# Hybrid encoder trunk on one core: four projection tiles instead of three side by side through the rows of x at the front

## The chip, the core and the metric

One Trainium2 chip, one of its cores. The core has TensorE (matmul, in the profile PE, its weight loads PEld), VectorE (DVE), ScalarE (ACT), GpSimd (POOL) and SyncE (SP, here the queue that issues nearly all DMAs), with SBUF and PSUM as its memories. The metric is the device time of one execution in microseconds (us); of a kernel, the median of several runs. One execution is also taken with the hardware profiler, and its span is what the profile divides up.

## The reference

One layer over 528 tokens (16 meta tokens ahead of 512 tokens of x), width 2048. All arithmetic is float32.

```python
h_res = concatenate([meta, x], axis=1)
hn = _rmsnorm(h_res, norm_in_g)
P = hn @ w_in                                   # 2048 x 8320
Pr, Pc = P[..., :RW_COLS], P[..., RW_COLS:]
prev = pad(Pr[:, :-1], one row at the top)
Pr = Pr + (prev - Pr) * mu_shift
r, k, v, g_r, wl, al = parts of Pr              # 4 x 1024, 64, 64
w_raw = -softplus(-(w0 + tanh(wl) @ w_lora_up)) - 0.5
decay = exp(-exp(w_raw)); a = sigmoid(a0 + al @ a_lora_up)
kk = k * k_k, normalised per head; k = k * (1 + (a - 1) * k_a)
y = _rwkv7_recurrence(r, decay, k, v, kk, kk * a)
y_a = (groupnorm(y) * lnx_g + lnx_b + bonus) * silu(g_r)
Bg, Cg, hc, g_c = parts of Pc                   # 4 x 1024
y_b = Bg * _causal_depthwise_conv(Cg * hc, conv_w) * silu(g_c)
h_res = h_res + concatenate([y_a, y_b]) @ w_out
out = _rmsnorm(h_res, norm_f_g)[:, N_META:]
```

The first RMS norm divides each token by a scale that depends on that token alone; the kernel multiplies the projections of the unscaled rows by it afterwards (`rs`).

## The kernel before

**Projections.** `w_in` is cut into 65 column tiles of 128: one of the low-rank inputs ("lora"), eight each of k, r, v, g (the RWKV half) and of B, C, h, gc (the convolution half). `plan` (line 105) is the order in which they are computed; `stream` holds each tile's weights as two halves of 128x1024. x lies transposed as 16 row blocks of 128 (`kt`), with all 528 tokens as columns. A tile is the sum over the 16 blocks, and for each block there are three matmuls: every float32 operand is split into a rounded part and its remainder (xh and xl for x, wh and wl for the weights), and hi x hi, hi x lo and lo x hi are added up in PSUM (`steps`, line 303). A tile's tokens lie in two PSUM banks (`FULL`: 2 x 264 columns, for lora, k, v; `TAIL`: 258 + 256, for r, g, C, h) or, where the meta tokens aren't wanted, in one (`REAL`: 512, for B and gc). So a FULL or TAIL tile takes 96 matmuls, a REAL tile 48 twice as wide.

**Splitting.** For weights ScalarE writes wh and VectorE (for odd quarters later in the stream GpSimd) writes wl = w - wh (`split_w`, lines 121 to 126; a quarter is 128x512 and covers four row blocks). Six buffers each hold wh and wl, three hold raw halves. For x, ScalarE writes xh (with the norm's gain) and VectorE xl (`split_x`, line 191). `square_x` squares a row block on ScalarE and adds it up on VectorE (`accd`, line 203), for the token scale.

**The front.** The first three tiles (lora, k0, r0) go side by side through the row blocks as these arrive: block by block in the first quarter (`quarters` 0, 2, 4, cut into pieces that come with the first blocks of x in one array, `front`), then quarter by quarter. The order of ScalarE and VectorE is written out by hand in this part (lines 239 to 261). In the last quarter, `token_scale_sums` (line 430) sums the squares over partitions by matmul into `pss`; VectorE scales (`var`), GpSimd takes the power -1/2 (line 101) and spreads it (`yb`, line 442); `token_scale` (line 445) transposes it on TensorE to `prs` and VectorE copies it to `rs`. The sums stand ahead of k0's last quarter, the transposes halfway through r0's; then lora and k0 are taken out of PSUM (`use`), r0 after its end.

**After the front** the program runs two things on TensorE, in one order fixed when the program is built. `mains` is the flow of the remaining projection tiles in `plan`'s order. `prepare` and `invert` do the chunked recurrence's set-up by pairs of heads: low-rank products (tz, ta), gram products (g), inversion in steps (t, z, t2, z2), and `recur` the recurrence. Between their steps `fill(ns)` runs so much of the flow, by a table of estimates, that the engines behind a step have time; `until(what, i)` runs the flow until a tile is there. DMAs of results are put off by `later(ns)`, measured in the flow's own estimated time. The other engines' orders come from a scheduler that knows priorities. SP issues the DMAs in one order: an entry whose buffer or data isn't ready holds those behind it.

**The convolution half.** For channel tile i, `use` takes C, then h (product on GpSimd, three taps on ScalarE and VectorE into `cv`), then B (out of PSUM into a rotating buffer `tm`, multiplied into cv on GpSimd), then gc.

Of the kernel before, what the change touches and what calls it, by code (L numbers as in the profile page):

```python
# [76 lines left out]
def hymba_kernel(ctx: ExitStack, tc: tile.TileContext, xt, xtok, front, w_in, w_out, pv, lup, cst, msk, gf, out):  # L77
# [27 lines left out]
    plan = [("lora", 0), ("k", 0), ("r", 0), ("v", 0), ("k", 1), ("r", 1), ("v", 1), ("g", 0), ("g", 1)]  # L105
    for j in range(0, NPAIR, 2):
        if j:
            plan += [(what, i) for i in (j, j + 1) for what in ("k", "r", "v")] + [("g", j), ("g", j + 1)]
        plan += [(what, j // 2) for what in ("C", "h", "B", "gc")]
# [5 lines left out]
    stream[0:6] = [stream[j] for j in (0, 2, 4, 1, 3, 5)]  # L115
# [12 lines left out]
    def prefetch(upto):  # L128
        while state["next"] < min(upto, len(stream) if chain else N_IN):
# [3 lines left out]
            with tc.high_priority(offset=WEIGHTS):  # L133
                for q in range(2):
                    split_w(2 * j + q, raw[:, q * 512 : (q + 1) * 512], nc.gpsimd if q and 8 < j < N_IN else nc.vector)
# [41 lines left out]
    def view(tag, n):  # L177
        dims = {
            "v": [P, LP], "vs": [P, NCH, CH], "ar": [P, NCH, 2, CH], "bk": [P, NCH, 3, CH], "g": [P, SEQ],
            "xT1": [P, NCH, CH], "e1": [P, NCH, CH + 1], "bt": [P, 2, NCH - 1, CH],  # L180
# [36 lines left out]
    for n in range(3):  # L217
# [3 lines left out]
    F0, F1 = KT + P + L, 5 * P + L  # L221
    fr = [view("bt", F0), view("bk", F1), view("gt0", 6 * P + 2 * L)]
# [5 lines left out]
    raw[0], raw[1] = fr[0][:, KT + P : F0], fr[1][:, 5 * P : F1]  # L228
    for k in range(2):
        raw[2 + k] = fr[2][:, 6 * P + k * L : 6 * P + (k + 1) * L]  # L230
    later_w = [load_w(0, "g")]
    load_x("gt1", 4, 4)
    later_w += [load_w(1, "xT1"), load_w(2, "e1")]
# [5 lines left out]
    with tc.manual_schedule(engines={mybir.EngineType.DVE, mybir.EngineType.Activation}):  # L239
# [3 lines left out]
        for n in (1, 2):  # L243
            split_piece(n, 0, fr[1][:, (n - 1) * P : n * P])
        for n in range(3):
            split_piece(n, P, fr[1][:, (n + 2) * P : (n + 3) * P])
        split_x(1)
        for n in range(3):
            split_piece(n, 2 * P, fr[2][:, 2 * n * P : 2 * (n + 1) * P])
        for kt in (2, 3):  # L250
            split_x(kt)
        split_w(1, later_w[0], nc.vector)
        for kt in range(4, 8):
            split_x(kt)
        square_x(2, True)
        for n in (1, 2):
            split_w(2 * n + 1, later_w[n], nc.vector)
        square_x(3)
# [3 lines left out]
    with tc.issue_after(head):  # L262
        state["next"] = 3
        prefetch(5)
# [112 lines left out]
    def use(what, i, ps):  # L377
# [18 lines left out]
        elif what == "h":  # L396
# [12 lines left out]
            got[what, i] = cv  # L409
        elif what == "B":  # L410
            cv = got["h", i]
            b = tm(f"b{i}")[:, 0:SEQ]
            with behind_of("split"):
                scaled(REAL, ps, b, META)
            nc.gpsimd.tensor_tensor(out=cv, in0=cv, in1=b, op=ALU.mult)
# [29 lines left out]
    def token_scale(yb):  # L445
        prs = pi.tile([P, 512], F32, tag="misc", name="prs")
        for j in range(4):
            nc.tensor.transpose(prs[:, j * P : (j + 1) * P], yb[:, j], ident)
        nc.vector.tensor_copy(rs[:, 0:512], prs)
        prs2 = pi.tile([P, 16], F32, tag="ser", name="prs2")  # L450
# [1024 lines left out]
```

## Time and profile before

| | |
|---|---|
| median of 3 runs | 1023.5 us (1021.72 to 1024.06) |
| profiled execution, its own time | 1021.34 us |
| its span | 1019.6 us |
| granted TensorE clock, mean | 0.998 |
| HBM read, written | 136.92 MB, 36.35 MB |
| first matmul on x; v0 begins | 4.45 us; 46.35 us |

A row of the timeline has the start in us, the duration in us, engine, line, operation, output<-inputs by the program's names (buffer numbers left out), shape, and, in brackets, how long the engine had stood idle and what ended that. A row of a table by stretches has the stretch, its length and then, for PE, PEld, DVE, ACT and POOL, the busy time and the number of instructions, then the granted clock, the DMA share and GB/s. Starts of matmuls that follow each other closer than their durations are usual: they are pipelined.

### The profile page before, as it was taken

The page shows a single profiled execution, that of the slowest core. Times are in us where ns is not written, and L with a number is a line of the kernel's source. Part 1 is how long each engine was busy: PE and PEld are TensorE (multiplying, and loading weights), DVE is VectorE, ACT ScalarE, POOL GpSimd, SP SyncE. Part 2 cuts the span into 40 slices and gives each one's busy share as a digit, 9 for nine tenths or more (in the row PEclk, how much of TensorE's full clock was granted, in tenths as well). Part 3 has the DMA queues.
Part 4 walks back from the last instruction along what each step waited for, and adds up shares of the span by engine and source line. Part 5 has one row for each costly group of instructions (what it writes and reads, how often), then busy time and mean ns, then how long its engine had stood idle before and what let it go on. Part 6 is the DMA issues. An engine that isn't in the chain of part 4 may idle for free.

```text
span 1019.6 us, 23707 instructions
## 1 busy us (share of the span) xinstructions
PE 1005.0 (99%) x9723; PEld 917.8 (90%) x9723; DVE 684.2 (67%) x1235; ACT 394.6 (39%) x727; POOL 274.7 (27%) x294
## 2 busy tenths in 40 slices
PE   9999999999999999999999999999999999999996
PEld 7899998999998999998999998889889897787885
DVE  7877765568655569654669653244555697999786
ACT  7544322534322434322424322222222335445453
POOL 0132323323232323232323222223332332005001
PEclk9999999999999999999999999999999999999999
DMA  9436386364864263853273846877672687695644
GB/s 315 146 106 167 84 219 189 98 166 103 214 171 138 84 168 102 216 150 117 83 178 100 209 139 180 299 225 235 194 229 86 197 272 189 168 320 138 173 124 165
DMA packets 184892, 174.82 MB, mean 171 GB/s; under 512 B 121552, under 2 KB 142672, under 8 KB 184400
## 3 DMA queue, kind: packets, MB, share of 16 engines
q1 hardware_dynamic: 182192, 164.40, 54.1%
q0 software_dynamic: 2304, 8.39, 4.8%
q8 instruction: 76, 1.25, 0.5%
q10 hardware_dynamic: 288, 0.52, 0.1%
q14 instruction: 32, 0.26, 0.1%
HBM read 136.92 MB, written 36.35 MB: 170 GB/s over the span
## 4 chain that ended last, share of the span: by engine, by line
PE 90%; DVE 4%; DMA 3%; ACT 1%; issue 1%; SPq 0%; DVEq 0%; POOL 0%; ACTq 0%
PE ps_v L312 9%; PE ps_h L312 9%; PE ps_g L312 9%; PE ps_B L312 9%; PE ps_gc L312 9%; PE ps_k L312 9%; PE ps_C L312 8%; PE ps_r L312 8%; PE M L1199 4%; PE P L1199 3%; PE Q L1199 2%; PE g L638 2%; DVE ol L1172 1%; PE zs L963 1%; PE zy L967 1%
## 5 line engine op out<-in xcount | busy, mean ns | idle before, releaser
L125 POOL TENSOR_TENSOR wl<-wr,wh 128x512 fp32r<-128x512 f32 x121 | 170.3, 1408 | 371.6 <-ACT wh L124 349.4
L124 ACT CAST wh<-wr 128x512 fp32r<-128x512 f32 x254 | 154.0, 618 | 299.1 <-PE ps_k L312 52.3
L125 DVE TENSOR_TENSOR wl<-wr,wh 128x512 fp32r<-128x512 f32 x133 | 98.9, 752 | 107.3 <-ACT wh L124 106.2
L312 PE MATMUL ps_v<-xh,wh 128*128 128x264 f32 x256 | 73.1, 286 | 0.0
L312 PE MATMUL ps_k<-xh,wh 128*128 128x264 f32 x256 | 73.0, 285 | 0.0
L312 PE MATMUL ps_h<-xh,wh 128*128 128x258 f32 (+1 forms) x256 | 72.9, 285 | 0.1
L312 PE MATMUL ps_k<-xh,wl 128*128 128x264 f32 x256 | 73.0, 285 | 0.0
L312 PE MATMUL ps_r<-xh,wl 128*128 128x258 f32 (+1 forms) x256 | 72.1, 282 | 0.7 <-DVE wl L125 0.7
L312 PE MATMUL ps_v<-xh,wl 128*128 128x264 f32 x256 | 72.7, 284 | 0.0
L312 PE MATMUL ps_v<-xl,wh 128*128 128x264 f32 x256 | 72.7, 284 | 0.0
L312 PE MATMUL ps_k<-xl,wh 128*128 128x264 f32 x256 | 72.6, 284 | 0.0
L312 PE MATMUL ps_C<-xh,wh 128*128 128x258 f32 (+1 forms) x256 | 72.6, 284 | 0.0
L312 PE MATMUL ps_g<-xl,wh 128*128 128x258 f32 (+1 forms) x256 | 72.4, 283 | 0.0
L312 PE MATMUL ps_h<-xh,wl 128*128 128x258 f32 (+1 forms) x256 | 72.2, 282 | 0.0
L312 PE MATMUL ps_r<-xh,wh 128*128 128x258 f32 (+1 forms) x256 | 72.1, 282 | 0.0
L312 PE MATMUL ps_C<-xl,wh 128*128 128x258 f32 (+1 forms) x256 | 72.0, 281 | 0.0
L312 PE MATMUL ps_r<-xl,wh 128*128 128x258 f32 (+1 forms) x256 | 72.0, 281 | 0.0
L312 PE MATMUL ps_g<-xh,wh 128*128 128x258 f32 (+1 forms) x256 | 72.0, 281 | 0.0
L312 PE MATMUL ps_h<-xl,wh 128*128 128x258 f32 (+1 forms) x256 | 71.9, 281 | 0.0
L312 PE MATMUL ps_g<-xh,wl 128*128 128x258 f32 (+1 forms) x256 | 71.9, 281 | 0.0
L312 PE MATMUL ps_C<-xh,wl 128*128 128x258 f32 (+1 forms) x256 | 71.9, 281 | 0.0
L312 PE MATMUL ps_B<-xl,wh 128*128 128x512 f32 x128 | 51.0, 399 | 0.0
(344 smaller groups left out, 3001.2 us busy)
## 6 DMA issues: line engine op xcount, KB each, us to landing
wr<-in_w_in_dram SPq DMA_DIRECT2D x127, 512.0 KB
ct<-opd SPq DMA_DIRECT2D x64, 288.0 KB
wo<-in_w_out_dram SPq DMA_DIRECT2D x24, 512.0 KB
x<-in_w_out_dram POOLq DMA_DIRECT2D x16, 512.0 KB, 5.6
opd<-ar SPq DMA_DIRECT2D x8, 576.0 KB
opd<-gt SPq DMA_DIRECT2D x16, 288.0 KB
opd<-bt SPq DMA_DIRECT2D x64, 64.0 KB
x<-in_w_out_dram SPq DMA_DIRECT2D x8, 512.0 KB
```

Of the source, the lines that this page charges most:

```text
L124: nc.scalar.copy(hi, rq)
L125: low[q] = eng.tensor_tensor(out=lo, in0=rq, in1=hi.bitcast(F32), op=ALU.subtract).ins
L312: nc.tensor.matmul(ps[r], ww[:, w], xx[:, kt, a:b], start=(kt == 0 and n == 0), stop=(kt == KT - 1 and n == 2))
L638: nc.tensor.matmul(z[h][:, c - c0], bk[hs, c, h : h + 2, :].rearrange("p a s -> p (a s)"), ar[hs, c].rearrange("p a s -> p (a s)"), start= ...
L963: nc.tensor.matmul(d[hs, j], w, x[hs], start=(a == 0), stop=(a == b - 1))
L967: nc.tensor.matmul(d[ho, j], t[hs, o : o + CH], x[hs], start=(a == 0), stop=(a == b - 1))
L1172: nc.vector.tensor_tensor(out=lo, in0=rq, in1=hi.bitcast(F32), op=ALU.subtract)
L1199: nc.tensor.matmul(bank[s], left(prod, jj, m, s), w, start=(jj == 0 and n == 0), stop=(jj == 7 and n == 2))
```

## The change

B0, the first tile of the convolution gate B, joins lora, k0 and r0 at the front and leaves its place behind h0 in `plan`. Its first quarter comes as pieces in `front` like those of the others, its second as a load of its own (`later_w`, four loads instead of three). The array `front` is now loaded in four parts instead of three, so that the pieces of block 0 come ahead of block 1. In ScalarE's and VectorE's order the split of block 1 stands ahead of the weight pieces of block 1, that of block 2 ahead of the pieces of blocks 2 and 3. The first block's matmuls on lora are ordered by operand: both banks with hi x xh, then lo x xh, then hi x xl.

B0's bank is the one that the tag "ser" has in PSUM. The meta rows' transpose, which had used it, goes to "misc" and stands halfway through B0's last quarter; lora and k0 are `use`d there. The sums of squares stand ahead of r0's last quarter instead of k0's. B0 is taken out of PSUM into an SBUF tile of its own, `b0`, and kept; its product with the convolution is made in `use("h", 0)`. All quarters of the first eleven halves (before: nine) of the stream are subtracted on VectorE.

```diff
@@ -102,17 +102,17 @@
 
 
     stream = []
-    plan = [("lora", 0), ("k", 0), ("r", 0), ("v", 0), ("k", 1), ("r", 1), ("v", 1), ("g", 0), ("g", 1)]
+    plan = [("lora", 0), ("k", 0), ("r", 0), ("B", 0), ("v", 0), ("k", 1), ("r", 1), ("v", 1), ("g", 0), ("g", 1)]
     for j in range(0, NPAIR, 2):
         if j:
             plan += [(what, i) for i in (j, j + 1) for what in ("k", "r", "v")] + [("g", j), ("g", j + 1)]
-        plan += [(what, j // 2) for what in ("C", "h", "B", "gc")]
+        plan += [(what, j // 2) for what in ("C", "h", "B", "gc") if j or what != "B"]
     plan += [(what, i) for i in range(4, NPAIR) for what in ("C", "h", "B", "gc")]
     tile_of = {"r": 0, "k": 8, "v": 16, "g": 24, "lora": 32, "B": 33, "C": 41, "h": 49, "gc": 57}
     for what, i in plan:
         m = tile_of[what] + i
         stream += [w_in[m, :, 0:1024], w_in[m, :, 1024:2048]]
-    stream[0:6] = [stream[j] for j in (0, 2, 4, 1, 3, 5)]
+    stream[0:8] = [stream[j] for j in (0, 2, 4, 6, 1, 3, 5, 7)]
     N_IN = len(stream)
     stream += [w_out[0, g] for g in range(3)]
     quarters, chain, low = {}, {}, {}
@@ -132,7 +132,7 @@
             state["dma"] = nc.sync.dma_start(raw, stream[j]).ins
             with tc.high_priority(offset=WEIGHTS):
                 for q in range(2):
-                    split_w(2 * j + q, raw[:, q * 512 : (q + 1) * 512], nc.gpsimd if q and 8 < j < N_IN else nc.vector)
+                    split_w(2 * j + q, raw[:, q * 512 : (q + 1) * 512], nc.gpsimd if q and 10 < j < N_IN else nc.vector)
             state["next"] = j + 1
 
     keep = ctx.enter_context(tc.tile_pool(name="keep", bufs=1, side="right"))
@@ -177,7 +177,7 @@
     def view(tag, n):
         dims = {
             "v": [P, LP], "vs": [P, NCH, CH], "ar": [P, NCH, 2, CH], "bk": [P, NCH, 3, CH], "g": [P, SEQ],
-            "xT1": [P, NCH, CH], "e1": [P, NCH, CH + 1], "bt": [P, 2, NCH - 1, CH],
+            "r0": [P, SEQ], "xT0": [P, NCH, CH], "xT1": [P, NCH, CH], "e1": [P, NCH, CH + 1], "bt": [P, 2, NCH - 1, CH],
         }.get(tag, [P, 2, NCH, P])
         t = cq.tile(dims, F32, tag=tag, name=f"in_{tag}")
         return bass.AP(tensor=t.tensor, offset=t.offset, ap=[list(t.ap[0]), [1, n]])
@@ -214,23 +214,23 @@
         nc.vector.tensor_tensor(out=lo[:, cols], in0=t, in1=hi[:, cols].bitcast(F32), op=ALU.subtract)
 
 
-    for n in range(3):
+    for n in range(4):
         quarters[2 * n] = tuple(
             wp.tile([P, 512], F32R, tag=tag, name=f"w{tag[0]}{2 * n}", bufs=6) for tag in ("hi", "lo")
         )
-    F0, F1 = KT + P + L, 5 * P + L
-    fr = [view("bt", F0), view("bk", F1), view("gt0", 6 * P + 2 * L)]
+    F0, F1, F2 = KT + P + L, 4 * P + L, 8 * P + 2 * L
+    fr = [view("bt", F0), view("r0", 3 * P), view("bk", F1), view("gt0", F2)]
     o = 0
     for t in fr:
         nc.sync.dma_start(t, front[:, o : o + t.shape[1]])
         o += t.shape[1]
     ng = fr[0]
-    raw[0], raw[1] = fr[0][:, KT + P : F0], fr[1][:, 5 * P : F1]
+    raw[0], raw[1] = fr[0][:, KT + P : F0], fr[2][:, 4 * P : F1]
     for k in range(2):
-        raw[2 + k] = fr[2][:, 6 * P + k * L : 6 * P + (k + 1) * L]
+        raw[2 + k] = fr[3][:, 8 * P + k * L : 8 * P + (k + 1) * L]
     later_w = [load_w(0, "g")]
     load_x("gt1", 4, 4)
-    later_w += [load_w(1, "xT1"), load_w(2, "e1")]
+    later_w += [load_w(1, "xT1"), load_w(2, "e1"), load_w(3, "xT0")]
     nc.scalar.activation(warm, warm, AF.Tanh)
     load_x("ar", 8, 2)
     load_x("v", 10, 1)
@@ -240,28 +240,30 @@
         split_piece(0, 0, fr[0][:, KT : KT + P])
         split_x(0, slice(0, L // 2))
         split_x(0, slice(L // 2, L))
-        for n in (1, 2):
+        for n in (1, 2, 3):
             split_piece(n, 0, fr[1][:, (n - 1) * P : n * P])
-        for n in range(3):
-            split_piece(n, P, fr[1][:, (n + 2) * P : (n + 3) * P])
         split_x(1)
-        for n in range(3):
-            split_piece(n, 2 * P, fr[2][:, 2 * n * P : 2 * (n + 1) * P])
+        for n in range(4):
+            split_piece(n, P, fr[2][:, n * P : (n + 1) * P])
         for kt in (2, 3):
             split_x(kt)
+            if kt == 2:
+                for n in range(4):
+                    split_piece(n, 2 * P, fr[3][:, 2 * n * P : 2 * (n + 1) * P])
         split_w(1, later_w[0], nc.vector)
         for kt in range(4, 8):
             split_x(kt)
+        split_w(3, later_w[1], nc.vector)
         square_x(2, True)
-        for n in (1, 2):
+        square_x(3)
+        for n in (2, 3):
             split_w(2 * n + 1, later_w[n], nc.vector)
-        square_x(3)
         square_x(0)
         square_x(1)
         head = split_x(8)
     with tc.issue_after(head):
-        state["next"] = 3
-        prefetch(5)
+        state["next"] = 4
+        prefetch(6)
         for kt in range(9, 12):
             split_x(kt)
             square_x(kt - 5)
@@ -407,12 +409,15 @@
                     out=cv, in0=u[:, j : j + SEQ], scalar=col(V_CW, 8 * j + i), in1=cv, op0=ALU.mult, op1=ALU.add
                 )
             got[what, i] = cv
+            if i == 0:
+                nc.gpsimd.tensor_tensor(out=cv, in0=cv, in1=got["B", 0], op=ALU.mult)
         elif what == "B":
-            cv = got["h", i]
-            b = tm(f"b{i}")[:, 0:SEQ]
+            b = tm(f"b{i}")[:, 0:SEQ] if i else tp.tile([P, SEQ], F32, name="b0")
             with behind_of("split"):
                 scaled(REAL, ps, b, META)
-            nc.gpsimd.tensor_tensor(out=cv, in0=cv, in1=b, op=ALU.mult)
+            got[what, i] = b
+            if i:
+                nc.gpsimd.tensor_tensor(out=got["h", i], in0=got["h", i], in1=b, op=ALU.mult)
         else:
             cv = got["h", i]
             g = tm(f"gc{i}")[:, 0:SEQ]
@@ -442,37 +447,53 @@
         nc.gpsimd.tensor_copy(yb, var[:, 1, 0:5].unsqueeze(2).to_broadcast([P, 5, P]))
         return yb
 
-    def token_scale(yb):
+    def token_scale(yb, part):
         prs = pi.tile([P, 512], F32, tag="misc", name="prs")
-        for j in range(4):
-            nc.tensor.transpose(prs[:, j * P : (j + 1) * P], yb[:, j], ident)
-        nc.vector.tensor_copy(rs[:, 0:512], prs)
-        prs2 = pi.tile([P, 16], F32, tag="ser", name="prs2")
-        nc.tensor.transpose(prs2, yb[0:META, 4], ident[0:META, 0:META])
-        nc.vector.tensor_copy(rs[:, 512:L], prs2)
+        if part == 0:
+            for j in range(4):
+                nc.tensor.transpose(prs[:, j * P : (j + 1) * P], yb[:, j], ident)
+            nc.vector.tensor_copy(rs[:, 0:512], prs)
+        else:
+            nc.tensor.transpose(prs[:, 0:META], yb[0:META, 4], ident[0:META, 0:META])
+            nc.vector.tensor_copy(rs[:, 512:L], prs[:, 0:META])
 
     def mains():
         pa = banks(FULL, "lora", pm, "main")
         pb = banks(FULL, "k0", pz, "tz")
         pc = banks(TAIL, "r0", pm, "main")
-        three = ((pa, FULL), (pb, FULL), (pc, TAIL))
+        pd = [pi.tile([P, SEQ], F32, tag="ser", name="ps_B0")]
+        four = ((pa, FULL), (pb, FULL), (pc, TAIL), (pd, REAL))
         for k in range(4):
-            for n, (ps, rg) in enumerate(three):
+            for n, (ps, rg) in enumerate(four):
+                if k == n == 0:
+                    hi, lo = quarters[0]
+                    for ww, xx, first in ((hi, xh, True), (lo, xh, False), (hi, xl, False)):
+                        for p, (a, b) in zip(ps, rg):
+                            nc.tensor.matmul(p, ww[:, 0:P], xx[:, 0, a:b], start=first, stop=False)
+                            yield (b - a) * 0.43
+                    continue
                 yield from steps(ps, rg, 0, 2 * n, (k,))
         for k4 in range(1, 4):
-            for n, (ps, rg) in enumerate(three):
-                h = 3 * (k4 // 2) + n
-                prefetch(h + 3)
-                if k4 == 3 and n == 1:
+            for n, (ps, rg) in enumerate(four):
+                h = 4 * (k4 // 2) + n
+                if k4 == 2:
+                    prefetch(h + 3)
+                if (k4, n) == (3, 2):
                     yb = token_scale_sums()
-                for r in range(2):
+                if (k4, n) == (3, 3):
+                    yield from steps(ps, rg, k4, 2 * h + k4 % 2, range(2))
+                    token_scale(yb, 4)
+                    use("lora", 0, pa)
+                    use("k", 0, pb)
+                    yield from steps(ps, rg, k4, 2 * h + k4 % 2, range(2, 4))
+                    continue
+                for r in range(2 if n < 3 else 1):
                     if (k4, n, r) == (3, 2, 1):
-                        token_scale(yb)
-                        use("lora", 0, pa)
-                        use("k", 0, pb)
+                        token_scale(yb, 0)
                     yield from steps(ps, rg, k4, 2 * h + k4 % 2, range(4), (r,))
         use("r", 0, pc)
-        for j in range(3, len(plan)):
+        use("B", 0, pd)
+        for j in range(4, len(plan)):
             what, i = plan[j]
             rg = FULL if what in ("k", "v") else REAL if what in ("B", "gc") else TAIL
             ps = yield from main(j, rg, f"{what}{i}")
@@ -1445,8 +1466,8 @@
     lup = np.stack([np.asarray(i[n])[0].reshape(64, 8, P) for n in ("w_lora_up", "a_lora_up")], 2)
     lup = np.concatenate([lup, lup], 0).transpose(1, 0, 2, 3)
 
-    first = [w[m, :, 0:512].reshape(P, 4, P) for m in (32, 8, 0)]
-    front = [pv[:, V_NG : V_NG + KT], first[0][:, 0], xt[:, 0], first[1][:, 0], first[2][:, 0]]
+    first = [w[m, :, 0:512].reshape(P, 4, P) for m in (32, 8, 0, 33)]
+    front = [pv[:, V_NG : V_NG + KT], first[0][:, 0], xt[:, 0]] + [t[:, 0] for t in first[1:]]
     front += [t[:, 1] for t in first] + [xt[:, 1]] + [t[:, 2:4].reshape(P, 256) for t in first] + [xt[:, 2], xt[:, 3]]
     front = np.concatenate(front, 1)
     cst, msk = _constants()
```

## The prediction

> **What bounds the kernel now.** The page comes first: which engine carries the span, and which carries the chain that ends last.
>
> ```profile
> span 1019.6 us, 23707 instructions
> PE 1005.0 (99%) x9723; PEld 917.8 (90%) x9723; DVE 684.2 (67%) x1235; ACT 394.6 (39%) x727; POOL 274.7 (27%) x294
> PE 90%; DVE 4%; DMA 3%; ACT 1%; issue 1%; SPq 0%; DVEq 0%; POOL 0%; ACTq 0%
> ```
>
> TensorE is busy for 99% of the span and carries 90% of the chain. No matmul is added or dropped by the change, so only what TensorE waits for can change the time. The list of its waits over the whole span (in total, times, longest, us) says where that is; these three rows are its front:
>
> ```profile
> PE ps_lora L312 <- DVE xl L194: 1.0, 2, 0.7
> PE pss L433 <- DVE accd L203: 0.9, 1, 0.9
> PE ps_r L312 <- DVE wl L125: 0.7, 1, 0.7
> ```
>
> There lora, k0 and r0 run side by side. Busy time hides part of such a loss, since a pipelined matmul counts as busy while it drains; so I read the losses from the distance between starts in the timeline of TensorE (start, duration, form):
>
> ```profile
> 4.45 0.72 PE L312 MATMUL ps_lora<-xh,wh 128*128 128x264 f32 x1
> 5.76 0.39 PE L312 MATMUL ps_k<-xh,wh 128*128 128x264 f32 x1
> 7.39 0.28 PE L312 MATMUL ps_lora<-xh,wh 128*128 128x264 f32 x1
> 8.23 0.28 PE L312 MATMUL ps_lora<-xh,wl 128*128 128x264 f32 x1
> 15.23 0.28 PE L312 MATMUL ps_lora<-xh,wh 128*128 128x264 f32 x1
> 16.39 0.28 PE L312 MATMUL ps_lora<-xh,wh 128*128 128x264 f32 x1
> 24.37 0.28 PE L312 MATMUL ps_lora<-xh,wh 128*128 128x264 f32 x1
> 26.29 0.29 PE L312 MATMUL ps_lora<-xh,wl 128*128 128x264 f32 x1
> 30.90 0.28 PE L312 MATMUL ps_r<-xl,wh 128*128 128x258 f32 x1
> 32.08 0.29 PE L312 MATMUL ps_r<-xh,wh 128*128 128x258 f32 x1
> 38.57 1.19 PE L433 MATMUL pss<-cs,accd 128*128 128x1 f32 x10 [0.92 <-DVE accd L203]
> 39.69 0.39 PE L312 MATMUL ps_k<-xh,wh 128*128 128x264 f32 x1
> 46.35 0.28 PE L312 MATMUL ps_v<-xh,wh 128*128 128x264 f32 x1
> 52.32 0.29 PE L528 MATMUL tz<-la,luh 128*128 128x272 f32 x1
> ```
>
> From 16.39 to 24.37 lie 66 matmuls, 0.121 us each: the pace without waits. Against it: the first six (4.45 to 5.76) lose 1.31 - 0.73 = 0.58; row block 1 of x (7.39 to 8.23, two steps) 0.60; block 7 (15.23 to 16.39, six) 0.43; blocks 10 and 11 (24.37 to 26.29, five) 1.31; the second half of r0's weights (30.90 to 32.08, two) 0.94; the sums of squares 0.92, the idle time of their row. Together 4.8 us; in each case x or weights are split too late for three tiles' pace.
>
> **The change part by part.** The fourth tile has half as many matmuls as the others, each about twice as wide. In its place of before:
>
> ```profile
> 147.77 0.40 PE L312 MATMUL ps_B<-xl,wh 128*128 128x512 f32 x1
> 158.59 0.39 PE L312 MATMUL ps_B<-xh,wl 128*128 128x512 f32 x1
> ```
>
> 46 steps lie between these two, 0.235 us each. B0 costs 48 x 0.235 = 11.3 us before and after; the change moves it. At the front it gives every row block of the first quarter 3 x 0.235 = 0.7 us more work, and every later quarter 2.8 us. The program order gives a clean schedule: quarter one ends at 5.6 + 2.2 + 3 x 2.88 = 16.4 (18 x 0.121 + 0.705 = 2.88 per block), then 72 x 0.121 + 12 x 0.235 = 11.5 per quarter: 27.9, 39.4.
>
> Is x in time for that? What feeds it:
>
> ```profile
> 4.42 0.90 DVE L194 SCALAR_TENSOR_TENSOR xl<-in_bt,xh 128x264 fp32r<-128x264 f32 x2
> 7.60 1.02 ACT L213 CAST wh<-in_gt 128x256 fp32r<-128x256 f32 x3 [0.45 <-DMA in_gt<-in_front_dram]
> 12.40 2.62 ACT L193 ACTIVATE xh<-in_gt,in_bt 128x528 fp32r<-128x528 f32 x4 [1.93 <-DMA in_gt<-in_xt_dram]
> 13.18 2.81 DVE L194 SCALAR_TENSOR_TENSOR xl<-in_gt,in_bt,xh 128x528 fp32r<-128x528 f32 x4 [1.83 <-ACT xh L193]
> 25.24 0.77 DVE L194 SCALAR_TENSOR_TENSOR xl<-in_vs,in_bt,xh 128x528 fp32r<-128x528 f32 x1
> 31.11 2.50 DVE L125 TENSOR_TENSOR wl<-wr,wh 128x512 fp32r<-128x512 f32 x4
> ```
>
> The front now loads 256 KB more ahead of row blocks 4 to 7. Between 7.60 and 12.40 a 256 KB and a 1056 KB load landed, 273 KB per us, so these blocks come 0.9 us later. VectorE also gets one more quarter to subtract ahead of blocks 8 to 15 (2.50 / 4 = 0.61 us a piece in a row); the added queue entries on SP cost less than that. Item by item:
> - First six: both halves of xh go first, then the two xl products, ready at 4.42 + 0.90 = 5.32. I take 0.2 gained (0 to 0.58).
> - Block 1: its split now stands before four weight pieces, not behind five of some 0.2 each, and so ends well ahead of the 8 us at which TensorE got it, though some 0.4 of landing (128 KB) is added; TensorE comes at 5.6 + 2.2 = 7.8. The 0.60 goes.
> - Block 7: done at 15.99 + 0.9 = 16.9, wanted at 17.6. The 0.43 goes.
> - Blocks 10 and 11: done at 26.0 + 0.9 + 0.6 = 27.5, block 11 wanted at 29.0. The 1.31 goes.
> - r0's second half: done at 31.72 + 0.9 + 0.6 = 33.2, wanted at 27.9 + 48 x 0.121 + 0.24 = 34.0. The 0.94 goes, with the thinnest cover, 0.8 us; if that is gone up to 0.94 comes back.
> - Sums: they stand one tile later, behind k0 instead of before it, at 39.4 + 5.8 = 45.3; VectorE's last addition (38.5 in this trace) is some 2 us later. The 0.92 goes.
> Removed: 0.2 + 0.60 + 0.43 + 1.31 + 0.94 + 0.92 = 4.40 us.
>
> Now what it adds. Before, k0's last quarter and half of r0's stood between the sums (38.57) and the transposes that need their result; now only half of r0's stands there. The chain between goes over VectorE (var) to GpSimd:
>
> ```profile
> 40.23 1.72 POOL L101 TENSOR_TENSOR var<-var,mhalf 128x8 f32<-128x8 f32 x1 [0.27 <-DVE var L437]
> 42.01 0.72 POOL L442 COPY yb<-var 128x640 f32<-128x640 f32 x1
> ```
>
> From the first sum to yb: 42.73 - 38.57 = 4.16 us, some 4.25 with the signal to TensorE (estimate). TensorE has 39.69 - 38.57 = 1.12 of sums, 0.1 of restart and 12 x 0.121 = 1.45 of r0: 2.67. So it stands before the transposes for **1.6 us**, a wait that this trace does not have, plus 0.1 for the restart. Behind it in order stand r0's other half, B0's last, then v0; VectorE's copies of lora and k0 out of their banks wait with it. The transpose of the 16 meta rows is now apart from the other four: another break, 0.1. Added: 1.8.
>
> The power (pow, line 101) now stands beside a subtraction of weights on VectorE (quarter 19). How such pairs fare:
>
> ```profile
> 243.61 1.84 DVE L616 TENSOR_TENSOR ta<-ta,k 128x576 f32<-128x576 f32 x1 [0.74 <-POOL ta L610]
> 243.54 1.29 POOL L125 TENSOR_TENSOR wl<-wr,wh 128x512 fp32r<-128x512 f32 x1
> 350.50 0.75 DVE L616 TENSOR_TENSOR ta<-ta,k 128x576 f32<-128x576 f32 x1
> ```
>
> The same VectorE instruction takes 0.75 alone and 1.84 where GpSimd had begun 0.07 before it; it ends 0.6 us after GpSimd does. If VectorE begins first, the power should pay up to one subtraction, 0.6. I take 0, since the order is tight, and keep 0.6 for the range. [...]
>
> Behind the front, B0's eviction now stands on VectorE ahead of lora's mixing, and waits for B0's end:
>
> ```profile
> 47.17 0.77 DVE L340 SCALAR_TENSOR_TENSOR lora_pre<-pr_lora,omm,sh_lora 128x528 f32<-128x528 f32 x1 [0.18 <-ACT sh_lora L338]
> 50.59 0.70 DVE L370 TENSOR_TENSOR la<-lora_al,la 64x528 fp32r<-64x528 f32 x1
> ```
>
> This chain takes 51.29 - 47.17 = 4.1 us and ends 1.0 before tz. After: eviction (0.7) and a subtraction (0.6) behind B0's end, 4.1, and 0.4 of r0's eviction between: 5.9 us, against some 6.0 from v0's start to tz (52.32 - 46.35). I take 0.1 (0 to 0.9).
>
> In the middle B0's 11.3 us leave the stretch before the first inversion, and all later projections come forward. The order shows where that is given back: 9 matmuls fewer ahead of tz2 (1.1 us), 24 ahead of tz3 (2.9), 27 of B's width ahead of k4 (6.3); from k4 on both orders are alike. I take 0.1 for tz2's bank (0 to 0.5). B0's multiplication moves to GpSimd behind the convolution, off TensorE's way.
>
> **Sum:** 4.40 - 1.8 - 0.2 = 2.4 us gained, 0.23%. The profiled execution took 1021.34 (span 1019.6), 2.16 under the median 1023.5; it would become 1018.9, the median 1021.1.
>
> **The rivals.**
> - *The covers are too thin.* VectorE has no room in the front (row below, 19.33 of 20 us), so r0's weights are late again (0.94), the power pays 0.6 and tz some 0.5. Gain 0.4: 1023.1. For it: 0.8 us of cover. Against: the covers of the other five are larger.
> - *Slower: the middle loses its cover.* Where 2.9 and 6.3 us of projections go from ahead of pairs 3 and 4, VectorE may set the pace, and TensorE's gram products wait.
>
> ```profile
> 20.00:40.00 20.00, 17.62 (x140) 16.75 (x139) 19.33 (x41) 15.53 (x29) 0.43 (x3) 1.00 0.70 219
> 227.00:253.00 26.00, 26.00 (x223) 25.86 (x223) 23.48 (x52) 10.25 (x20) 8.86 (x12) 1.00 0.48 124
> 316.00:338.00 22.00, 22.00 (x205) 20.33 (x192) 8.27 (x17) 5.91 (x10) 4.85 (x5) 1.00 0.44 136
> 248.48 0.69 DVE L622 TENSOR_TENSOR ar<-r,e 128x512 f32<-128x512 f32 x1
> 252.43 0.83 PE L638 MATMUL g<-ar,bk 64*128 64x128 f32 x10
> ```
>
> The third number pair after the length is VectorE. For it: 23.48 of 26 us at pair 3. Against: ar is done at 249.2, 3.3 us ahead of the products, and before k4 VectorE is busy for only 8.27 of 22. It decides once VectorE is over 3.3 us late. If both stretches are lost whole, 9.2 - 2.4 = 6.8 us slower: 1030.3; half of them: 1025.7.
> - *Hidden anyway.* The end is set by something clocked apart from TensorE, and the front's gain is waited away: 1023.5. Against: 99% busy and 90% of the chain.
>
> **How the numbers follow.** Forecast 0.56 (1021.1), thin covers 0.26, middle 0.13, hidden 0.05. The runs of before spread over 1021.7 to 1024.1, so some 0.2% (2 us) is what can be told from no change, and the forecast is not far over it. Its own range, 1019.3 to 1022.4, is the gain with its bounds (3.0 down to 1.1) and part of the spread; 1018.5 to 1024.6 takes in the thin covers with noise and the smallest of the slow cases. Faster by over 0.2%: 0.56; within: 0.30; slower: 0.14.
>
> **What would show it.** TensorE's list of waits should lose its rows for xl, wl and accd in the first 60 us and gain one of prs for yb, 1.4 to 2.3 us; v0 should begin near 54.6 (46.35 + 11.3 = 57.6 without a gain), and all shared marks from the recurrence on should stand 2 to 3 us earlier. A row for ps_r behind wl, or for tz behind la, shows the thin covers; one for g behind ar or bk near 240 or 345 the slow rival. If the front gains 3 us and the end none, the third rival holds.

## The result, and the profile after

The changed kernel takes 1025.44 us (median of 11 runs, 1023.54 to 1027.53), the kernel before 1022.60 us in runs beside it. The ratio is 1.0026, with a 95% interval of 1.0016 to 1.0037: slower by some 2.7 us, where 2.4 us less was forecast. The profiled execution took 1025.44 us. Its page, and below it TensorE's list of waits (total, times, longest, us):

```profile
span 1023.6 us, 23708 instructions
PE 1006.6 (98%) x9723; PEld 919.0 (90%) x9723; DVE 686.1 (67%) x1239; ACT 393.8 (38%) x729; POOL 273.8 (27%) x292
```

```profile
PE t L831 <- DVE xn L822: 2.2, 1, 2.2
PE prs L454 <- POOL yb L447: 1.7, 1, 1.7
PE pwarm L173 <- DVE cold L170: 1.4, 1, 1.4
PE ps_k L314 <- DVE wl L125: 1.1, 1, 1.1
```

The three rows of the front that the prediction quoted are gone, and the one that it forecast, prs for yb, is there. But two rows are new that it has not: t for xn, and ps_k for wl. The front in the timeline:

```profile
47.56 1.98 POOL L101 TENSOR_TENSOR var<-var,mhalf 128x8 f32<-128x8 f32 x1 [0.28 <-DVE var L442]
...
50.38 0.66 PE L454 MATMUL prs<-cs,yb 128*128 128x128 f32 x4 [1.66 <-POOL yb L447]
...
55.41 0.28 PE L314 MATMUL ps_v<-xh,wh 128*128 128x264 f32 x1
...
61.55 0.39 PE L549 MATMUL tz<-la,luh 128*128 128x272 f32 x1
```

v0 begins at 55.41, not at the 57.6 (46.35 + 11.3) of a front that gains nothing: 2.2 us are won. From here TensorE's order can be compared mark by mark. How much later than in the profile of before each mark starts (difference of the starts in the two timelines, us; "end" is the last group of matmuls):

| kernel | tz, pair 0 | t, 1st inversion | tz, pair 3 | t, 2nd inversion | tz, pair 4 | end |
|---|---|---|---|---|---|---|
| changed | +9.23 | +10.72 | +6.15 | +5.95 | +3.49 | +3.94 |
| place only (below) | +12.59 | +13.99 | +9.41 | +9.20 | +5.32 | +5.16 |
| place, mended (below) | +11.11 | +11.09 | +6.51 | +6.30 | -0.12 | +2.81 |
| h1 late (below) | +9.79 | +11.30 | +6.71 | +6.51 | +0.11 | +0.61 |
| both late (below) | +9.60 | +9.68 | +5.10 | +4.90 | -1.51 | +0.14 |
| all (below) | +7.66 | +7.75 | +3.16 | +2.96 | -3.44 | -2.55 |

B0's 11.3 us stand at the front and are handed back until pair 4. At the first mark the changed kernel is 2.07 us to the good (11.3 - 9.23); at pair 4, where both orders are alike again, it is 3.49 behind. So 5.56 us are lost in the middle, at two places. The first is in this stretch of the timeline (VectorE, then TensorE's row between):

```profile
168.19 0.69 DVE L333 TENSOR_TENSOR gc<-ps_gc,rs 128x512 f32<-128x512 f32 x1 [6.40 <-PE ps_gc L314]
168.79 0.68 DVE L125 TENSOR_TENSOR wl<-wr,wh 128x512 fp32r<-128x512 f32 x1
169.53 0.39 PE L314 MATMUL ps_k<-xh,wl 128*128 128x264 f32 x1 [1.14 <-DVE wl L125]
170.99 3.48 DVE L125 TENSOR_TENSOR wl<-wr,wh 128x512 fp32r<-128x512 f32 x2
174.40 0.70 DVE L822 STREAM_TRANSPOSE xn<-xT 128x512 f32<-128x512 f32 x1
```

The scaling of gc0 waits on VectorE until TensorE has ended that tile, and the split of k2's first weights stands behind it, though it could have run in the 6.40 us of idle time. TensorE goes on to k2 and finds no wl. In the profile of before, gc0 was handled only behind the first inversion's transposes:

```profile
161.94 0.70 DVE L801 STREAM_TRANSPOSE xn<-xT 128x512 f32<-128x512 f32 x1
...
175.13 0.69 DVE L331 TENSOR_TENSOR gc<-ps_gc,rs 128x512 f32<-128x512 f32 x1
```

The tile ahead of them was B0, whose scaling the program puts behind the next tile's split (`behind_of("split")`). The second place in the changed kernel:

```profile
298.28 0.42 DVE L333 TENSOR_TENSOR hh<-ps_h,rs 128x256 f32<-128x256 f32 x1 [0.97 <-PE ps_h L314]
298.78 1.29 POOL L404 TENSOR_TENSOR u<-u,hh 128x514 f32<-128x514 f32 x1 [9.41 <-DVE hh L333]
300.11 0.72 ACT L406 ACTIVATE cv<-u,pvt 128x512 f32<-128x512 f32 x1 [8.87 <-POOL u L404]
300.74 2.17 ACT L124 CAST wh<-wr 128x512 fp32r<-128x512 f32 x4
300.87 1.54 DVE L408 SCALAR_TENSOR_TENSOR cv<-u,pvt,cv 128x512 f32<-128x512 f32 x2 [2.17 <-ACT cv L406]
302.32 3.45 DVE L125 TENSOR_TENSOR wl<-wr,wh 128x512 fp32r<-128x512 f32 x2
302.00 3.23 POOL L125 TENSOR_TENSOR wl<-wr,wh 128x512 fp32r<-128x512 f32 x2 [1.92 <-ACT wh L124]
305.70 0.70 DVE L822 STREAM_TRANSPOSE xn<-xT 128x512 f32<-128x512 f32 x1
306.45 1.14 PE L831 MATMUL t<-xn,gt 64*64 64x64 f32 x32 [2.24 <-DVE xn L822]
```

And in the profile of before:

```profile
295.75 0.71 DVE L801 STREAM_TRANSPOSE xn<-xT 128x512 f32<-128x512 f32 x1 [1.20 <-DMA xT<-sx]
297.57 1.16 PE L810 MATMUL t<-xn,gt 64*64 64x64 f32 x64
...
302.21 1.27 POOL L402 TENSOR_TENSOR u<-u,hh 128x514 f32<-128x514 f32 x1
```

Read it from the bottom. t waits for a transpose on VectorE. Ahead of that in VectorE's queue stand two splits, and ahead of these the convolution's two taps (300.87). The taps wait for the convolution's first product on ScalarE (300.11), and the four casts that write wh for the splits stand behind the same product. ScalarE had been idle for 8.87 us in front of it, until GpSimd had u, and GpSimd until h1 was out of PSUM. In the kernel before, h1 lay across the inversion, so that its handling came behind the transposes (u at 302.21, t at 297.57). In the changed kernel h1 is complete 23 B matmuls before t, and its whole chain stands in front. Each of the two splits takes 1.73 us beside GpSimd's, where the one at 168.79 takes 0.68: the kind of pair that the prediction quoted at 243.5.

Behind the wait comes a third loss. The trace records the granted clock in steps of 3.41 us, counted from where it first rises (5.96 us in this profile; from there it is full for 88 steps and then half for one). By those windows (stretch, length, PE, PEld, DVE, ACT and POOL busy, granted clock, DMA share, GB/s):

```profile
302.93:306.34 3.41, 1.28 (x35) 0.74 (x33) 3.41 (x3) 0.00 (x0) 2.55 (x3) 1.00 0.27 65
306.34:309.75 3.41, 3.30 (x37) 2.77 (x38) 0.56 (x2) 2.11 (x4) 0.00 (x0) 0.50 0.89 288
```

The window with the wait has TensorE busy for 1.28 of 3.41 us, and the next one runs at half clock. From the second inversion's t to pair 4's tz the mended kernel (below) hands back 6.4 us of B0's, the changed kernel 2.5, so it loses 4.0 us there. The wait and its restart are 2.5 of these, which is what the place-only kernel loses there with no half clock behind its wait; the half clock is then some 1.5 us. With the 1.5 us at k2 (from 9.23 to 10.72 in the table) that is 5.5 of the 5.56 us.

### The profile page after: what moved, and what is told of

It is laid out like the page before. It is cut to its first block, busy times and chain, and to the rows that moved or that the text cites. A ratio compares the mean times of both kernels' runs of the same rounds, so it can differ in the third digit from the quotient of the medians.

```text
span 1023.6 us, 23708 instructions
## 1 busy us (share of the span) xinstructions
PE 1006.6 (98%) x9723; PEld 919.0 (90%) x9723; DVE 686.1 (67%) x1239; ACT 393.8 (38%) x729; POOL 273.8 (27%) x292
## 4 chain that ended last, share of the span: by engine, by line
PE 68%; DVE 8%; DMA 4%; issue 2%; SPq 1%; ACT 1%; POOL 0%; DVEq 0%; ACTq 0%; POOLq 0%
PE ps_gc L314 8%; PE ps_h L314 8%; PE ps_B L314 7%; PE ps_k L314 7%; PE ps_v L314 7%; PE ps_C L314 7%; PE ps_g L314 7%; PE ps_r L314 7%; DVE ol L1193 3%; DMA wo<-in_w_out_dram 2%; PE M L1220 2%; PE g L659 1%; PE zs L984 1%; PE Q L1220 1%; DVE xb L1201 1%
## 5 line engine op out<-in xcount | busy, mean ns | idle before, releaser
L314 PE MATMUL ps_B<-xh,wl 128*128 128x512 f32 x128 | 51.3, 401 | 0.0
```

Of the source, the lines that this page charges most:

```text
L314: nc.tensor.matmul(ps[r], ww[:, w], xx[:, kt, a:b], start=(kt == 0 and n == 0), stop=(kt == KT - 1 and n == 2))
```

## The experiments

Ratios are to the kernel before, with runs beside it on the same chip, and 95% intervals.

**gc0's scaling behind the next split.**

```diff
-            if what == "B" and i < 4:
+            if (what == "B" and i < 4) or (what, i) == ("gc", 0):
                 state["split"] = low[4 * j + 4]
...
-            scaled(REAL, ps, g, META)
+            with behind_of("split"):
+                scaled(REAL, ps, g, META)
```

> The changed kernel, with one order alone altered: the scaling of the first gc tile (L333, 0.69 us on VectorE) is put behind the first weight split of the next tile, k2, as the scalings of B tiles already are. Theory A (two waits in the middle, made by two in-order queues, eat the front's gain): the wait of 1.14 us of k2's matmuls for wl goes, nothing takes its place, and about 1.1 of the 2.8 us lost comes back: 1024.3 us, ratio to the kernel before 1.0016. Rival B (VectorE as a whole sets the pace of the middle, as the slow case of the prediction had it): moving one scaling by one place leaves VectorE's work as it was, the wait turns up at the next product that needs VectorE, and the time stays at 1025.4 us. Rival C (the granted clock, 0.996 in place of 0.998, is the loss, and the waits are covered): 1025.4 us as well, but with no new wait on TensorE.

Measured: 1025.38 us, ratio 1.0016 (1.0007 to 1.0025). The waits of its profile:

```profile
PE t L832 <- DVE xn L823: 2.9, 2, 2.2
PE prs L455 <- POOL yb L448: 1.7, 1, 1.7
```

ps_k's wait is gone, and t at the first inversion starts 1.4 us earlier, measured from tz; but the row of t has a second wait, 0.65 us, at that inversion: the gate's chain still stood ahead of the transpose. The ratio is the one forecast, but it is a miss in part: a wait did take the old one's place, from there on 0.84 us of the 1.4 are lost again, and the interval reaches into that of the changed kernel, so the medians alone show no gain.

**h1 handled behind the second inversion's transposes.**

```diff
+            if (what, i) == ("h", 1) and "turned2" not in state:
+                state["late"] = lambda ps=ps: use("h", 1, ps)
+                continue
             use(what, i, ps)
...
                 nc.scalar.copy(ts_[e], z[e])
+        if first == 2:
+            state["turned2"] = True
+            if "late" in state:
+                state.pop("late")()
         fill(FW["lev"])
```

> The changed kernel, with the handling of tile h1 (its scaling on VectorE, the product on GpSimd, the convolution) held back until the second inversion's transposes stand in the queues, as it was by chance in the kernel before. Theory A: the wait of t for xn, 2.24 us, goes or falls under 0.5 us; and if that pause is what lowers the granted clock to half for the next 3.4 us, that goes too, another 1.7 us: 1021.5 us, ratio 0.999, granted clock back at 0.998. Rival C (the clock is lowered by something else, and by chance): the wait goes but the clock does not come back, 1023.2 us. Rival B: the wait moves to the gram products of pairs 2 and 3 and the time stays at 1025.4 us. What could spoil it: ScalarE may now have the convolution's first product ahead of ts, which would show as a wait of z for ts of up to 2 us.

Measured: 1021.14 us, ratio 0.9984 (0.9975 to 0.9994), granted clock 0.998. The second inversion in its timeline:

```profile
301.14 0.71 DVE L825 STREAM_TRANSPOSE xn<-xT 128x512 f32<-128x512 f32 x1 [3.86 <-DMA xT<-sx]
302.57 1.29 POOL L404 TENSOR_TENSOR u<-u,hh 128x514 f32<-128x514 f32 x1 [1.54 <-DVE hh L333]
303.90 0.72 ACT L406 ACTIVATE cv<-u,pvt 128x512 f32<-128x512 f32 x1 [4.50 <-POOL u L404]
304.08 1.16 PE L834 MATMUL t<-xn,gt 64*64 64x64 f32 x64
```

The transpose now waits for its data alone, t does not wait, and between the second inversion's t and its next level 3.94 us come back, as the theory said (2.24 + 1.7). This one order, in TensorE's unchanged order of matmuls, turns the change from slower to faster.

**The sums one tile earlier.**

```diff
-                if (k4, n) == (3, 2):
+                if (k4, n) == (3, 1):
                     yb = token_scale_sums()
```

> The changed kernel, with the sums of squares taken one tile earlier (ahead of k0's last quarter in place of r0's), the place relative to the transposes that the kernel before has. accd is complete at 39.7 us, 3.4 us before the new place at 43.1, so the sums should not wait; the 1.66 us wait of prs for yb should go. Theory A (the front's wait lies on the path): 1.66 us less, 1023.8 us, ratio 1.0010. Rival (a later start of the middle is given back at the next wait, so what the front gains is not kept): 1025.4 us, with the middle's two waits longer by the same 1.7 us.

Measured: 1022.59 us, ratio 0.9994 (0.9985 to 1.0003). The wait of prs is gone; tz of pair 0 comes 1.35 us earlier than in the changed kernel (the fronts of single profiles differ by up to 0.6 us, as the first column of the table shows for kernels with the same one). The ratio falls by more than that, by 0.3%, though the two intervals (1.0016 and up, 1.0003 and down) also allow the 0.13% that 1.35 us are; and 1.0003 doesn't rule out that this kernel only equals the kernel before. In this profile the 2.24 us wait at the second inversion is still there, but lies across two windows of the clock's grid, and neither is followed by half clock. Whether early sums do that regularly, no run shows:

```profile
300.73:304.14 3.41, 2.13 (x39) 1.46 (x37) 3.41 (x3) 0.84 (x2) 3.40 (x3) 1.00 0.20 64
304.14:307.55 3.41, 2.44 (x40) 2.07 (x41) 1.00 (x3) 1.71 (x4) 0.00 (x0) 1.00 0.74 237
```

**The place alone.** The kernel before, with B0 as an ordinary tile behind r0:

```diff
-    plan = [("lora", 0), ("k", 0), ("r", 0), ("v", 0), ...
+    plan = [("lora", 0), ("k", 0), ("r", 0), ("B", 0), ("v", 0), ...
-        plan += [(what, j // 2) for what in ("C", "h", "B", "gc")]
+        plan += [(what, j // 2) for what in ("C", "h", "B", "gc") if j or what != "B"]
...
-        fill(FW["start"] if i else 6700)
+        fill(FW["start"] if i else 6700 + 10568 + FW["evac"])
```

with `b0` kept and multiplied in `use("h", 0)` as in the changed kernel.

> The kernel before with its three-tile front, and tile B0 alone moved: it runs as an ordinary tile right behind r0, and the first pair's chain begins as much later as in the changed kernel, so that from v0 on TensorE's order is the changed kernel's, row for row. No part of the new front is in it. Theory A (the place that B0 leaves in the middle costs, whatever the front does): the wait of 1.1 us at k2 and that of 2.2 us at the second inversion appear with the half clock behind it, 5.0 us in all, up to 6.0 by the offsets between the two profiles: 1027.6 to 1028.6 us, ratio 1.005 to 1.006. Rival D (the four-tile front itself leaves work behind, loads or splits, that the middle pays for): 1022.6 us, and no such waits. Rival B: slower too, but with the waits at the gram products.

Measured: 1027.12 us, ratio 1.0036 (1.0024 to 1.0049).

```profile
PE t L813 <- DVE xn L804: 2.2, 1, 2.2
...
PE ps_k L312 <- DVE wl L125: 1.1, 1, 1.1
```

Both waits are here with nothing of the new front, and none at a gram product: theory A, and neither rival. The size is below the forecast; in this profile no half clock followed the wait (its windows are quoted in the last section), and of the other runs there is no trace. In the table of marks it loses 1.4 us at k2 and 2.5 at the second inversion against its mended twin, below. That it stands 1.5 us behind the twin at pair 0 already is another window at half clock, in the old front (last section).

**A wait of the same length, put into the kernel before.**

```diff
             for q in both:
+                for _ in range(6 if q and first == 2 else 1):
                     state["turned"] = nc.vector.transpose(
```

> The kernel before, with one thing added: the last transpose ahead of the second inversion's t is run six times instead of once (five more at 0.71 us, 3.55 us, of which 1.1 us is slack), so that t waits 2.4 to 2.6 us for xn, about as in the changed kernel, while nothing else is moved. Theory A with the clock on a fixed grid of 3.41 us (in the profiles a window of that grid with 62% and one with 66% of it empty on TensorE were followed by one at half clock, windows with 49%, 47% and 37% were not): the time rises by 2.5 us and by 1.7 us more in those runs where the wait falls mostly into one window; in the profile the half window is there if one window is empty for 62% or more, and not at 49% or less. 1025.1 to 1026.8 us. Rival (the half clock comes from something else in the changed kernel): 1025.1 us and the clock never lower behind the wait.

Measured: 1025.72 us, ratio 1.0023 (1.0012 to 1.0033); t waits 1.9 us, less than the 2.4 to 2.6 expected. The windows:

```profile
297.86:301.27 3.41, 1.56 (x39) 1.49 (x40) 2.64 (x5) 1.45 (x3) 0.00 (x0) 1.00 1.03 399
301.27:304.68 3.41, 3.41 (x12) 2.73 (x11) 0.60 (x2) 1.58 (x3) 2.25 (x2) 0.50 0.32 121
```

The half clock follows at 54% empty, between the two shares that the expectation gave, and from t to the next level 3.67 us are lost, twice the wait. So the wait alone brings it, with nothing else of the changed kernel. The medians lie only 2.6 us apart; some runs may lack that window, and runs of the kernel before lose one too (last section).

**The same, longer** (`range(9 ...)`).

> As the run before it, with the transpose run nine times; two of the queue's other instructions come in between, so that t waits 4.6 to 5.3 us. Theory A with the grid: whatever the grid's phase, one window of 3.41 us is then empty for two thirds or more, so the half clock follows in each run: 4.6 to 5.3 us of wait and 1.7 us of clock, 6.3 to 7.0 us in all, 1028.9 to 1029.6 us. Rival: the wait alone, 1027.2 to 1027.9 us.

Measured: 1029.78 us, ratio 1.0064 (1.0049 to 1.0078); t waits 4.7 us.

```profile
297.13:300.54 3.41, 0.80 (x34) 0.56 (x32) 3.31 (x6) 0.62 (x1) 0.00 (x0) 1.00 0.99 364
300.54:303.95 3.41, 1.36 (x33) 1.25 (x34) 2.24 (x4) 0.19 (x1) 0.00 (x0) 0.50 0.76 286
303.95:307.36 3.41, 3.41 (x13) 3.10 (x13) 0.43 (x1) 1.50 (x3) 0.88 (x1) 0.50 0.00 0
```

Two windows at half clock behind two thin ones, and 7.0 us lost for a wait of 4.7.

**Both handled late,** gc0 behind the first inversion's transposes, h1 behind the second's; the front as in the changed kernel.

```diff
+    held, inverted = {}, set()
...
+            if ((what, i) == ('gc', 0) and 0 not in inverted) or ((what, i) == ('h', 1) and 2 not in inverted):
+                held[what, i] = ps
+                continue
             use(what, i, ps)
...
                 nc.scalar.copy(ts_[e], z[e])
+        inverted.add(first)
+        for key in list(held):
+            use(*key, held.pop(key))
...
-            scaled(REAL, ps, g, META)
+            with behind_of("turned"):
+                scaled(REAL, ps, g, META)
```

> The changed kernel with both middle orders altered and the front left as it is: h1's handling behind the second inversion's transposes as in the run before, and gc0's handling in the same way behind the first inversion's. TensorE's order is unchanged. In the run with gc0 moved by one place alone, TensorE stood 1.4 us earlier up to the first inversion and lost 0.84 of it there: 0.65 us of t waiting for xn, because the gate's chain and two splits of 1.7 us each still stood ahead of that transpose. Theory A: with the whole chain behind the transpose, neither wait is left, 1.4 us come on top of the 3.9 us of the late h1: 1025.4 less 5.3 is 1020.1 us, ratio to the kernel before 0.9975. Rival: the 1.4 us cannot be had, since what follows (z for ts, or the next splits) waits in its place: 1021.3 us, as with h1 alone, ratio 0.9985.

Measured: 1020.34 us, ratio 0.9971 (0.9960 to 0.9983). In the table of marks the 1.4 us at the first inversion are kept this time, and at pair 4 it stands 5.0 us ahead of the changed kernel.

**All three:** the sums early, gc0 and h1 late.

> All three at once: sums one tile earlier, h1 and gc0 behind the transposes. Theory A, sum of the parts as the single runs showed them in the trace: 1.35 us in the front, 1.4 at the first inversion, 3.9 at the second: 1025.4 less 6.65 is 1018.8 us, ratio 0.9960 to 0.9965, below the kernel before by 3.5 to 4 us, of which 2.1 us is what the four-tile front itself brought. Rival (what is gained ahead of the recurrence is given back there, as the run with early sums lost 1.1 us of its 2.8 there, waiting for transfers): 1020 us, ratio 0.9975.

Measured: 1018.29 us, ratio 0.9947 (0.9935 to 0.9960), the best of all here, 5.4 us under the kernel before. What TensorE still waits for:

```profile
PE pwarm L173 <- DVE cold L170: 1.4, 1, 1.4
PE M L1228 <- DVE ol L1201: 0.8, 2, 0.5
PE ps_h L314 <- issue: 0.7, 1, 0.7
```

**The place alone, mended.** The place-only kernel with the edits of "both late".

> The kernel before with its three-tile front and B0 alone moved to its new place, as in the earlier run of the place alone, and with the handling of gc0 and of h1 held behind the transposes. TensorE's order is that of the earlier run, row for row. Theory A (the place costs only through the two queue orders): the earlier run's two waits, 1.1 and 2.2 us, and what stands behind them go, 4.1 us by its trace from the first low-rank product to that of pair 4, with the half clock left out; ratio to the kernel before 0.9995 to 1.0005 instead of 1.0036. Rival (the place costs in another way too, by buffers, transfers or the gram products): part of the 0.36% stays, ratio above 1.0015.

Measured: 1023.13 us, ratio 0.9995 (0.9986 to 1.0005). In the table B0's 11.1 us are handed back whole by pair 4 (-0.12). Once the queues are in order the place costs nothing that these runs can tell (by the interval 0.05% at most, where the place alone cost 0.24% at least): the loss was theirs.

**The changed kernel again.**

> The changed kernel itself once more, to set the others beside it on a second chip. All theories: ratio to the kernel before 1.002 to 1.004. By theory A its profile shows the 2.2 us wait of t for xn again, and a half clock behind it only if one window of the grid is empty for more than 55% or so; the window in the front where prs waits 1.7 us stays below that.

Measured: 1025.65 us, ratio 1.0019 (1.0010 to 1.0027), a little under the range expected. The waits of t and ps_k are there again (2.2 and 1.1 us), and by its marks (9.71 us later than before at pair 0, 4.03 at pair 4) the middle loses 5.6 us again.

```profile
303.67:307.08 3.41, 1.17 (x42) 0.70 (x44) 3.21 (x3) 0.00 (x0) 2.29 (x3) 1.00 0.38 114
307.08:310.49 3.41, 3.41 (x38) 2.81 (x36) 0.69 (x1) 2.11 (x4) 0.24 (x1) 0.50 0.87 238
```

## Why the prediction was wrong

**The front was right** in its mechanism, and a little high in size. All three rows of waits went, the wait of prs came at 1.66 us against 1.6 forecast, the power paid 0.26 us of the 0.6 at most (1.98 against 1.72), tz came 0.17 later behind v0 (6.14 against 5.97) where 0.1 was taken. Forecast 2.4 us, measured 2.07 at pair 0; in the other profiles with this front pair 0 is 9.60 to 9.79 us later than before, which makes it 1.5 to 1.7. Two of its sums are off without weight: by 4.40 less 1.8 v0 should have begun at 55.0, not near 54.6, and the chain to tz adds up to 5.8 us, not 5.9. The early sums show that the 1.66 us need not have been paid: in the changed kernel accd's last addition starts at 39.0, long before the sums at 46.0.

**The step that failed** is the passage on the middle: "In the middle B0's 11.3 us leave the stretch before the first inversion ... I take 0.1 for tz2's bank (0 to 0.5)". It followed TensorE's order alone, and rightly found that order handing B0's time back. (Its three amounts add up to 10.3 us, not 11.3; in the mended kernel 4.6 us come back from the first inversion to pair 3 and 6.4 from the second to pair 4, where it counted 4.0 and 6.3. That was not the failure.) What it left out is that with all projections 11.3 us earlier, two tiles end on the other side of an inversion: gc0 ahead of the first, h1 ahead of the second. Their handling then enters VectorE's, ScalarE's and GpSimd's queues ahead of the transposes. The measured price of that term, taken at 0.1 us, is 5.56 us in the profile, of which 4.0 is wait and restart (shown by the place-only kernel against its mended twin) and the rest half clock. The order of VectorE and ScalarE is fixed when the program is built, so it could have been compared before the run: by the timelines hh and cv stand ahead of the transpose in one kernel and behind it in the other.

**The slow rival** named the right sign and in part the right stretch (the second wait stands between pairs 3 and 4, the first ahead of pair 2), but not the mechanism. It had VectorE short of time, with the gram products waiting; in the changed kernel no gram product waits, and VectorE was idle for 6.40 us right ahead of the first wait. Its condition (ar 3.3 us late) did not come about, and that its 1025.7 us lies near the result is chance. The bounds were too low for the same reason: the range reached into this rival by "the smallest of the slow cases", not by a price of a late transpose, which then cost its own wait and some 1.5 us of clock besides.

**Hidden anyway** falls: with the queues mended, the front's gain reaches the end. Both late against place mended is 0.9971 against 0.9995, 2.5 us (by the intervals 0.3 to 4.6). In the marks of these two profiles it is 1.5 us at pair 0 and 1.4 at pair 4; what the old front loses in clock in many runs (last section) may be the rest, which no run separates. **Thin covers** falls too: r0's weights were in time.

One thing stays open. Between pair 4 and the end the profiles differ by up to 3 us: place mended loses 2.9 there, in three steps between 640 and 770 us, in the recurrence. The two profiles of the changed kernel itself lose 0.45 and 1.2, and the kernel with the wait of 1.9 us, in which B0 did not move, 0.5, so at least part of it comes and goes with the same program. Waits for operand transfers, 0.4 to 1.0 us in the lists, are part of it. I did not follow it further, so single profiles are compared up to pair 4 and the ends by medians.

## What to carry to other kernels

When a piece of work is moved in a program with in-order queues, list for each engine what now stands on the other side of every hard wait, not only for the engine that bounds the kernel. Here one scaling on VectorE and one product on ScalarE, each put in front of something that TensorE wanted sooner, cost more than the change brought (5.56 us in the profile against 2.07). A consumer that can wait (a gate, a convolution) should be put behind the producers of the critical step by an explicit order: that it stood there before was an accident of where its tile ended.

## What the runs showed of the hardware that was not expected

A short wait cost twice its length: with the added wait of 1.9 us 3.67 us were lost. In these profiles the clock is granted in windows of 3.41 us, and where TensorE was busy for 0.80, 1.17, 1.28, 1.36 or 1.56 us of one, the next ran at half clock; with 1.66 (both late, from 1009.8 us), 1.72, 1.79, 2.13 and 2.44 it did not. So the dividing line lies between 1.56 and 1.66 us in these profiles, at 46 to 49% of a window, and the same wait of 2.2 us falls on one side or the other by where it meets the grid (1.28 us busy in the changed kernel, 1.72 in the place-only kernel). The grid's phase differs from run to run: the clock first rises 4.3 to 7.2 us after the start. Two windows of the place-only kernel and one of the changed kernel (prs):

```profile
36.10:39.51 3.41, 2.49 (x22) 2.27 (x21) 2.99 (x10) 0.62 (x1) 0.00 (x0) 1.00 0.21 84
39.51:42.92 3.41, 3.41 (x17) 3.39 (x18) 0.55 (x3) 0.00 (x0) 2.72 (x5) 0.50 0.60 192
...
305.75:309.16 3.41, 1.72 (x37) 1.12 (x35) 3.41 (x3) 0.43 (x1) 2.99 (x3) 1.00 0.19 56
309.16:312.57 3.41, 2.85 (x42) 2.38 (x43) 1.00 (x2) 2.11 (x4) 0.00 (x0) 1.00 0.78 233
```

```profile
46.93:50.34 3.41, 1.79 (x15) 1.55 (x14) 0.81 (x3) 0.00 (x0) 2.85 (x5) 1.00 0.30 94
50.34:53.75 3.41, 3.38 (x23) 2.83 (x23) 2.16 (x4) 0.62 (x1) 0.13 (x2) 1.00 0.17 65
```

The first pair is an exception: busy for 2.49 us, and yet followed by half clock. That window has 0.92 us of wait and then most of the sums' products of one column; without these TensorE is busy for 1.45 us of it. In the four other profiles with the old front, the windows there keep 1.79 us or more without these products, and full clock follows. Without the products the first pair's window lies below the line too; whether they are the cause, no run tested. The new front, with 1.75 us or more in its thinnest window, lost none in any profile.

The kernel before does lose a window in many of its runs. In its profile the clock, once risen, falls to half only after the last matmul, and the mean of the granted clock is 0.998; in all these profiles that last stretch is 2.9 to 5.9 us long, which alone leaves a mean of 0.997 or more. In 39 of the 69 runs of the kernel before that stand beside the experiments the mean is 0.996 or less, in none of the 25 of "h1 late", "both late" and "all". Its one profile is thus among its fastest runs, and differences to it come out larger than those of the medians (3.94 us at the end for the changed kernel, against 2.7). That the window is the one in the old front is not shown.
